# Ordinary products for the first four up chunks of a feed-forward stage, and norm sums added on VectorE

## The chip, the cores and the metric

The kernel runs on one core of a Trainium2 chip. The metric is the device time of one execution in microseconds (us). The kernel before takes 2769.68 us, the median of three runs (2767.59 to 2777.74). All durations below come from one profiled execution of it. TensorE is PE in the profile, VectorE is DVE, ScalarE is ACT, GpSimd is POOL, and SyncE, which issues the DMAs, is SP.

## The reference, cut to what matters

Two transformer blocks run one after the other, each two layers deep, on 512 tokens of width 1024, all in float32:

```
x = x + mixer(rms_norm(x, g_mix)) 
x = x + square(relu(rms_norm(x, g_ffn) @ w_ff1)) @ w_ff2     # 1024 -> 4096 -> 1024
rms_norm(x, g) = x * rsqrt(mean(x*x, axis=-1) + 1e-6) * g
```

The first block's mixer joins a pooling branch, a latent attention and a linear recurrence through gates (twice). The second block has a layer with retention and window attention ("even") and one with axial attention ("odd"). Each of the four layers ends in such a feed-forward stage (ffn), so there are four of them, and eight norms over the width.

## The kernel before

Activations lie transposed, 128 of the 1024 channels on the partitions and the 512 tokens along the row; `xs[d]` (tile `zg`) is the residual of channel chunk d. TensorE takes each float32 operand as a rounded part and a rest, `xh` and `xl` for activations, `h` and `lo` for weights, and `mm3` (L412 to L415) forms a product from three matmuls: hi by hi, hi by lo, lo by hi. A norm's factor is not multiplied into x ahead of the product: x times its gain is split at once (`split_x`), and the factor of each token is applied to the product.

**Weights** come as 439 slabs of 512 KB. `fetch` (L369 ff.) issues the DMA on SP into a raw buffer (three of them), ACT rounds it to `h` (L394) and DVE subtracts to get `lo` (L395); for 38 slabs POOL does that. `ahead` keeps three slabs fetched in front of the one in use.

**The norm's statistic.** `Sum.add` squares a chunk of x on ACT (L470) and adds it to `ssq` on POOL (L421, called from L474). `tokens` (L481) multiplies `ssq` with ones on TensorE, so that each token's sum lies on its own partition, and DVE scales it (`tm`, L484). `rsqrt` makes 1/sqrt by three Newton steps on DVE, eleven operations on 128x4. `bcast` turns the result into a row for all partitions: two rounded diagonal tiles (`ssp`, DVE, L418), two matmuls with ones (L514), a copy by ACT (L517, `r2b` in an ffn, `rb` in a mixer). In the mixers `getr` does the statistic and the broadcast in one call, inside the first products.

**The up product.** Up chunk f is 128 of the 4096 columns. An ordinary chunk (`gemm`) is 8 x 3 matmuls of 512 tokens. The ffn before never uses that: a `Pair` handles two chunks by seven half-size products p1 to p7 (a Winograd scheme of the 2x2 blocks: halves of the contraction by halves of the tokens), 7 x 4 x 3 = 84 matmuls of 256 tokens. It needs seven forms of the weights, made by `fetch_up` (L341: five splits `sh`, `sl` and four sums or differences on DVE, for each pair), and seven of x, made by `split_up` (L532) at the end of the product before the ffn (`w_out`, or the mixers' out-projection), together with that product's own additions (`zg`), the squares and the POOL adds. `xh` holds the first token half and a difference in its even chunks; `th`, `tl` hold three more forms.

**The order.** The ffn calls pairs 0 and 1 first, with `tokens` after the first four products of pair 0 and `bcast` among pair 1's, then per group of four chunks two pairs and four down slabs (`ff2`). `tc.high_priority(offset=60)` moves what it holds 60 steps forward. The scheduler writes one fixed queue for each engine when the kernel is built; each engine works its queue in order. Accumulators in PSUM: three `ps_acc`, two `ps_s`, two `ps_tr`, one `ps_o`.

Of the kernel before, what the change touches and what calls it, by code (L numbers as in the profile page):

```python
# [16 lines left out]
S = 512  # L17
D = 1024
# [281 lines left out]
def build(tc, a, upto=None):  # L300
# [35 lines left out]
    for i, sl in enumerate(plan):  # L336
        if sl[0] and sl[0][0] in ("w_ff1", "w_mlp_up_2") and i - 1 not in ups:
            ups[i] = True
    up = {}

    def fetch_up():  # L341
# [18 lines left out]
        for src in (a1, b1, s1, a2, b2):  # L360
            fh = up["p"].tile([P, 4, P], F32R, name="sh", bufs=8)
            fl = up["p"].tile([P, 4, P], F32R, name="sl", bufs=8)
# [44 lines left out]
    def ahead():  # L407
        while pos[0] < min(len(plan), pos[1] + AHEAD):
            fetch()
# [52 lines left out]
    class Sum:  # L462
# [4 lines left out]
        def add(self, src, scale=None, eng=None):  # L467
# [5 lines left out]
            if self.n:  # L473
                add(self.s, self.s, dst, eng or nc.gpsimd)  # L474
            self.n += 1

        def tokens(self, n, eps=EPS, tag="s"):

            t = ps(tag)
            for b in range(NB):  # L480
# [3 lines left out]
            nc.vector.tensor_scalar(m, t[:, 0:2 * NB].rearrange("p (b t) -> p b t", t=2)[:, :, 0], 1.0 / n, eps,  # L484
                                    op0=ALU.mult, op1=ALU.add)
# [5 lines left out]
    def rsqrt(m, n=NB):  # L491

        i, y, t = nrm.tile([P, n], I32, name="ti%d" % n, bufs=2), small("ty%d" % n, n), small("tt%d" % n, n)
# [10 lines left out]
    def bcast(cols, out=None, tag="o", name="rb"):  # L504

        hl = [nrm.tile([P, NB], F32R, name=n, bufs=2) for n in ("bh", "bl")]
        nc.vector.tensor_copy(hl[0], cols)
        nc.vector.tensor_sub(hl[1], cols, hl[0].bitcast(F32))
        dg = nrm.tile([P, 2, S], F32R, name="ssp")
        t = ps(tag)  # L510
        for i in range(2):
            mul(dg[:, i].rearrange("p (b t) -> p b t", b=NB), identb,
                hl[i].bitcast(F32)[:, :, None].to_broadcast([P, NB, P]))
# [3 lines left out]
        nc.scalar.activation(out, t, AF.Copy)  # L517
# [13 lines left out]

    def split_up(d, src, g, mk):  # L532

        i, odd_ = divmod(d, 2)
        x = mk()
        nc.scalar.activation(x, src, AF.Copy, scale=g)
        if not odd_:
            t = mk()  # L540
            nc.vector.tensor_sub(t[:, 0:H], x[:, H:], x[:, 0:H])
            split(xh[:, d, 0:H], xl[:, d, 0:H], x[:, 0:H])
            split(xh[:, d, H:], xl[:, d, H:], t[:, 0:H])
            up["even"] = (x, t)
            return
        xe, t = up["even"]
        split(xh[:, d], xl[:, d], x)
        t2 = mk()
        nc.vector.tensor_sub(t2[:, 0:H], x[:, H:], t[:, 0:H])
        nc.vector.tensor_sub(t2[:, H:], x[:, 0:H], t2[:, 0:H])  # L550
        nc.vector.tensor_sub(t[:, H:], x[:, H:], xe[:, H:])
        th, tl = up["th"][:, i], up["tl"][:, i]
        split(th[:, 1:3], tl[:, 1:3], t2.rearrange("p (a b) -> p a b", a=2))
        split(th[:, 0], tl[:, 0], t[:, H:])
# [23 lines left out]


    def ffn(n1, n2, l, xs, sq, after):  # L580

        with contextlib.ExitStack() as st:
# [20 lines left out]
            class Pair:  # L606
# [32 lines left out]
                def out(self):  # L639
                    r = rb[0]  # L640
                    for j, t in enumerate(self.t):
                        stt(t, t, 0.0, r, op0=ALU.max)
                        yf = tp.tile([P, S], F32, name="yf", bufs=2)
                        nc.scalar.activation(yf, t, AF.Square)
                        y = yp.tile([P, 2, S], F32R, name="y")
                        nc.scalar.activation(y[:, 0], t, AF.Square)  # L646
                        nc.vector.tensor_sub(y[:, 1], yf, y[:, 0].bitcast(F32))  # L647
                        ys[2 * self.p + j] = y
# [15 lines left out]
            ahead()  # L664
            a0.mm("p3")
            a1 = Pair(1)
            a1.mm("p1")
            a0.mm("p4")
            a1.mm("p6")
            with tc.high_priority(offset=60):  # L670
                rb.append(bcast(y, tag="acc", name="r2b"))
            a0.out()
            a1.mm("p7", "p5", "p3", "p2")
            ahead()
            nxt = Pair(2)
            nxt.mm("p1")
            a1.mm("p4")
            a1.out()
            for j in range(1, KF // 4 + 1):
                for e in range(2):  # L680
                    c = None
                    if j < KF // 4:
                        c = nxt or Pair(2 * j + e)
                        c.mm(*(("p6", "p7") if nxt else ("p1", "p6", "p7")))
                        nxt = None
                    ff2(j - 1, 2 * e)
                    if c:
                        c.mm("p5", "p3", "p2")
# [10 lines left out]
    def mixer1(l, getr, xsrc, xs, mkpool):  # L699
# [14 lines left out]
        with contextlib.ExitStack() as st:  # L714
# [259 lines left out]
        with contextlib.ExitStack() as st:  # L974
# [19 lines left out]
            for d in range(KD):  # L994
# [5 lines left out]
                split_up(d, xs[d], vc("g_ffn", 8 * l + d), mm_)  # L1000
# [134 lines left out]
    def even(getr, xs, finish):  # L1135
# [6 lines left out]
        with contextlib.ExitStack() as st:  # L1142
# [4 lines left out]
            with tc.high_priority(offset=60):  # L1147
                rb, later = getr()
# [14 lines left out]
            for h in range(RH):  # L1163
# [10 lines left out]
                for i in range(2):  # L1174
                    acc = gemm(slab(_gemm(e, 0, _rng(R_G + 256 * h + P * i))))
# [372 lines left out]
```

## Time and profile before

| what | us |
|---|---|
| median of three runs | 2769.68 |
| the profiled execution | 2771.13 |
| its span | 2769.3 |
| PE busy in the span | 2692.5 (97%) |
| DVE busy | 2079.8 (75%) |
| ACT busy | 1289.1 (47%) |
| POOL busy | 272.7 (10%) |

An engine's busy time is the union of its instructions' durations. PE's matmuls overlap in the trace, so the pace of a run of them is the distance between two starts, not a duration. The granted clock (PEclk in a view by windows) is 1.00 at TensorE's full clock of 2.4 GHz and 0.50 at 1.2 GHz; a mean between the two says what share of the window each level had. The ffn stages begin at about 370, 1088, 1848 and 2415 us, the second mixer of the first block at 716, the even layer at 1425, the odd one at 2205.

### The profile page before, as it was taken

Reading aid. Unit: us, or ns where it says so; the run is one execution under the profiler, and the core shown is the slowest. Engines: PE = TensorE matmul, PEld = TensorE weight load, DVE = VectorE, ACT = ScalarE, POOL = GpSimd, SP = SyncE. Lnnn points to the kernel's source line nnn. Section 1 sums busy time; section 2 is a strip of 40 time slices with the busy share of each in tenths; the row PEclk is TensorE's granted clock in tenths of the full one; section 3 lists DMA queues with packets and bytes.
Section 4 is the critical chain, followed back from the end, with each engine's and each line's share of the span. In section 5 each row is a group of like instructions: output and inputs, shape, how many; then the busy total and the mean of one; then the engine's idle time right before and its main releaser. Section 6 shows DMA issues by size and latency. Waiting matters only on the chain. (4 is left out here: it accounts for less than half of the span.)

```text
span 2769.3 us, 38564 instructions
## 1 busy us (share of the span) xinstructions
PE 2692.5 (97%) x14774; PEld 2307.0 (83%) x14774; DVE 2079.8 (75%) x3925; ACT 1289.1 (47%) x2112; POOL 272.7 (10%) x186
## 2 busy tenths in 40 slices
PE   8999999999999999999999989989999999999999
PEld 6887889999777778999978878869999877789998
DVE  8647798777775779887766665688788676798775
ACT  4437654343354675443443335564434346644332
POOL 0100010000110002000031112330000132300000
PEclk9999999999999999999999999999999999999999
DMA  4331433332434223323322222213332311132332
GB/s 160 105 109 54 130 105 109 103 103 92 127 112 147 73 85 121 122 92 108 106 76 83 82 71 74 70 46 119 102 99 94 98 62 38 39 107 92 108 106 69
DMA packets 80481, 262.88 MB, mean 95 GB/s; under 512 B 9223, under 2 KB 13063, under 8 KB 80296
## 3 DMA queue, kind: packets, MB, share of 16 engines
q1 hardware_dynamic: 80296, 260.41, 29.4%
q8 instruction: 116, 1.90, 0.3%
q14 instruction: 69, 0.57, 0.1%
HBM read 248.06 MB, written 12.32 MB: 94 GB/s over the span
## 5 line engine op out<-in xcount | busy, mean ns | idle before, releaser
L394 ACT ACTIVATE h<-w 128x1024 fp32r<-128x1024 f32 (+1 forms) x313 | 329.7, 1055 | 700.5 <-issue 287.8
L413 PE MATMUL ps_acc<-y,h 128*128 128x512 f32 x1024 | 399.6, 391 | 0.0
L415 PE MATMUL ps_acc<-y,lo 128*128 128x512 f32 x1024 | 399.4, 390 | 0.0
L414 PE MATMUL ps_acc<-y,h 128*128 128x512 f32 x1024 | 399.1, 390 | 0.0
L395 DVE TENSOR_TENSOR lo<-w,h 128x1024 fp32r<-128x1024 f32 (+1 forms) x275 | 342.0, 1245 | 45.8 <-ACT h L394 43.2
L421 DVE TENSOR_TENSOR zg<-zg,ps_acc 128x512 f32<-128x512 f32 x304 | 207.3, 684 | 194.6 <-PE ps_acc L415 194.4
L413 PE MATMUL ps_acc<-xh,h 128*128 128x512 f32 x752 | 302.3, 402 | 0.0
L415 PE MATMUL ps_acc<-xh,lo 128*128 128x512 f32 x752 | 302.3, 402 | 0.0
L414 PE MATMUL ps_acc<-xl,h 128*128 128x512 f32 x752 | 302.0, 402 | 0.0
L415 PEld LDWEIGHTS ps_acc<-y,lo 128*128 128x128 f32 x1024 | 192.2, 188 | 41.1
L413 PEld LDWEIGHTS ps_acc<-y,h 128*128 128x128 f32 x1024 | 192.5, 188 | 37.5 <-ACT y L646 1.1
L414 PEld LDWEIGHTS ps_acc<-y,h 128*128 128x128 f32 x1024 | 192.3, 188 | 36.7 <-DVE y L647 0.8
L421 POOL TENSOR_TENSOR ssq<-ssq,sq 128x512 f32<-128x512 f32 x55 | 103.1, 1874 | 974.9 <-ACT sq L470 516.3
L413 PE MATMUL ps_tr<-xh,h 128*128 128x256 f32 (+1 forms) x544 | 166.8, 307 | 15.6 <-ACT xh L429 8.5
L414 PE MATMUL ps_tr<-xl,h 128*128 128x256 f32 (+1 forms) x544 | 165.7, 305 | 6.8 <-DVE xl L430 6.8
L430 DVE TENSOR_TENSOR sl<-w,sh 128x512 fp32r<-128x512 f32 x256 | 168.8, 682 | 3.6 <-ACT sh L429 3.4
L415 PEld LDWEIGHTS ps_acc<-xh,lo 128*128 128x128 f32 x752 | 143.5, 191 | 32.3 <-issue 1.7
L413 PEld LDWEIGHTS ps_acc<-xh,h 128*128 128x128 f32 x752 | 143.4, 191 | 32.2 <-issue 1.9
L414 PEld LDWEIGHTS ps_acc<-xl,h 128*128 128x128 f32 x752 | 143.6, 191 | 30.9 <-issue 0.8
L415 PE MATMUL ps_tr<-xh,lo 128*128 128x256 f32 (+1 forms) x544 | 166.5, 306 | 0.1
L429 ACT ACTIVATE sh<-w 128x512 fp32r<-128x512 f32 x256 | 151.1, 619 | 29.2 <-DVE w L357 15.2
L414 PE MATMUL ps_s<-tl,sh 128*128 128x256 f32 x480 | 136.5, 284 | 0.7 <-DVE tl L430 0.7
(422 smaller groups left out, 6671.6 us busy)
## 6 DMA issues: line engine op xcount, KB each, us to landing
w<-w SPq DMA_DIRECT2D x439, 512.0 KB, 3.6
md<-gz SPq DMA_DIRECT2D x16, 256.0 KB, 2.5
m<-md SPq DMA_DIRECT2D x16, 256.0 KB, 4.1
x0t<-xT SPq DMA_DIRECT2D x8, 256.0 KB, 6.4
m<-xT SPq DMA_DIRECT2D x8, 256.0 KB, 3.8
xd<-zg SPq DMA_DIRECT2D x8, 256.0 KB, 2.1
m<-xd SPq DMA_DIRECT2D x8, 256.0 KB, 3.9
out<-zg SPq DMA_DIRECT2D x8, 256.0 KB, 2.0
```

Source lines behind the costliest of these rows:

```text
L394: nc.scalar.activation(h[:, c], w[:, c], AF.Copy)
L395: (nc.gpsimd if idle(i) else nc.vector).tensor_sub(lo[:, c], w[:, c], h[:, c].bitcast(F32))
L413: nc.tensor.matmul(out, w[0], x[0], start=first, stop=False)
L414: nc.tensor.matmul(out, w[0], x[1], start=False, stop=False)
L415: nc.tensor.matmul(out, w[1], x[0], start=False, stop=last)
L421: (eng or nc.vector).tensor_add(out, x, y)
L429: nc.scalar.activation(hi, src, AF.Copy)
L430: nc.vector.tensor_sub(lo, src, hi.bitcast(F32))
```

## The change

It has four parts.

1. **Chunks 0 to 3 of each ffn are ordinary products.** Two chunks by `gemm2` (two accumulators side by side), one `gemm`, the broadcast, one more `gemm`. The pairs begin with pair 2. `split_up` is gone: the product before an ffn ends with the plain `split_x`. The forms of x are made by `forms` while the four chunks run, and at last the difference is written over the second token half of the even chunks of `xh`, `xl`.
2. **Pair 2's slabs are held back** (`up["hold"]`) until the second chunk has been squared; the rings `sh` and `sl` have 7 buffers, not 8; in the later rounds p5 comes ahead of the first down slab.
3. **`Sum.add` adds on DVE.** The 55 adds of `ssq` and 4 of `sqq` leave POOL; 7 of another sum (`sg`) stay there.
4. **Statistic and broadcast apart.** `getr` ends with the Newton steps; `bcast` is called later: after the fourth product in the first block's mixer, and in the even layer after two products for the gates of head 0 that are moved up for this. In the odd layer the broadcast, whose result nobody read, is gone. The small DVE operations, the diagonals and ACT's copy run at high priority.

```diff
@@ ffn_plan
-    out = up(0) + up(1)
+    out = [_gemm(n1, l, _rng(f * P)) for f in range(4)]
@@ ahead
-        while pos[0] < min(len(plan), pos[1] + AHEAD):
+        while pos[0] < min(len(plan), pos[1] + AHEAD) and not (up.get("hold") and pos[0] in ups):
@@ Sum.add
-                add(self.s, self.s, dst, eng or nc.gpsimd)
+                add(self.s, self.s, dst, eng)
@@ bcast
-        nc.vector.tensor_copy(hl[0], cols)
-        nc.vector.tensor_sub(hl[1], cols, hl[0].bitcast(F32))
         dg = nrm.tile([P, 2, S], F32R, name="ssp")
+        with tc.high_priority(offset=60):
+            nc.vector.tensor_copy(hl[0], cols)
+            nc.vector.tensor_sub(hl[1], cols, hl[0].bitcast(F32))
+            for i in range(2):
+                mul(dg[:, i].rearrange("p (b t) -> p b t", b=NB), identb,
+                    hl[i].bitcast(F32)[:, :, None].to_broadcast([P, NB, P]))
@@ ffn
+            def forms(i):
+                e, o = xs[2 * i], xs[2 * i + 1]
+                ge, go = gx(2 * i), gx(2 * i + 1)
+                half = lambda name, bufs: tp.tile([P, H], F32, name=name, bufs=bufs)
+                t1 = half("t1", 4)
+                nc.vector.tensor_sub(t1, e[:, H:], e[:, 0:H])
+                nc.scalar.activation(t1, t1, AF.Copy, scale=ge)
+                e2 = half("m1", 2)
+                nc.scalar.activation(e2, e[:, H:], AF.Copy, scale=ge)
+                t = tp.tile([P, S], F32, name="t", bufs=4)
+                stt(t[:, 0:H], o[:, H:], go, t1, op1=ALU.subtract)
+                stt(t[:, H:], o[:, 0:H], go, t[:, 0:H], op1=ALU.subtract)
+                t3 = half("u2", 2)
+                stt(t3, o[:, H:], go, e2, op1=ALU.subtract)
+                split(th[:, i, 1:3], tl[:, i, 1:3], t.rearrange("p (a b) -> p a b", a=2))
+                split(th[:, i, 0], tl[:, i, 0], t3)
+                return t1
...
-            a0 = Pair(0)
-            a0.mm("p1", "p5", "p2", "p6")
-            with tc.high_priority(offset=60):
-                y = rsqrt(sq.tokens(D, tag="acc"))
-            a0.mm("p7")
...
+            up["hold"] = True
+            ws = [slab(_gemm(n1, l, _rng(f * P))) for f in range(2)]
+            accs = gemm2(*ws)
+            y = rsqrt(sq.tokens(D))
+            t1s = [forms(0)]
+            accs.append(gemm(slab(_gemm(n1, l, _rng(2 * P)))))
+            rb.append(bcast(y, name="r2b"))
+            for f in range(4):
+                if f == 1:
+                    accs.append(gemm(slab(_gemm(n1, l, _rng(3 * P)))))
+                if f:
+                    t1s.append(forms(f))
+                t = tp.tile([P, S], F32, name="t", bufs=4)
+                stt(t, accs[f], 0.0, rb[0], op0=ALU.max)
+                square(f, t)
+                if f == 1:
+                    up["hold"] = False
+                    ahead()
+            for i, t1 in enumerate(t1s):
+                split(xh[:, 2 * i, H:], xl[:, 2 * i, H:], t1)
@@ mixer1
-            with tc.high_priority(offset=60):
-                rb = getr()
+            y = getr()
             accs.append(gemm(slab(slab_in(l, POOL0 + P))))
+            rb = bcast(y)
@@ even
-            with tc.high_priority(offset=60):
-                rb, later = getr()
+            gate = lambda h, i: gemm(slab(_gemm(e, 0, _rng(R_G + 256 * h + P * i))))
+            gacc = [gate(0, 0)]
+            y, later = getr()
+            gacc.append(gate(0, 1))
+            rb = bcast(y)
@@ odd
-        with tc.high_priority(offset=60):
-            rb, later = getr()
+        rt_, later = getr()
```

The queues of three places follow. DVE, at the first ffn's broadcast, before (`w_3457`, `w_3458` and the `sl` are the weight forms of pair 2, `ssp` the diagonals, `t_3400` a result of pair 0):

```order
577 L358 TENSOR_TENSOR w_3457<-w_3457 128x512
578 L507 CAST bh_3548<-ty4_3428 128x4
579 L421 TENSOR_TENSOR u2_3546<-ps_s_3533,m1_3517 128x256
580 L430 TENSOR_TENSOR sl_3471<-w_3457,sh_3470 128x512
581 L508 TENSOR_TENSOR bl_3549<-ty4_3428,bh_3548 128x4
582 L430 TENSOR_TENSOR sl_3475<-w_3458,sh_3474 128x512
583 L418 TENSOR_TENSOR ssp_3552<-ident_85,bh_3548 128x512
584 L430 TENSOR_TENSOR sl_3479<-s1_3464,sh_3478 128x512
585 L418 TENSOR_TENSOR ssp_3552<-ident_85,bl_3549 128x512
586 L430 TENSOR_TENSOR sl_3483<-w_3457,sh_3482 128x512
```

And now, in the changed kernel (`sl_3458` is the last weight form of pair 2, `lo_3582` the rest of the second down slab, `xl_88` the difference written over `xl`):

```order
550 L430 TENSOR_TENSOR sl_3458<-w_3429,sh_3457 128x512
551 L418 TENSOR_TENSOR tt4_3312<-ty4_3311 128x4
552 L395 TENSOR_TENSOR lo_3582<-w_3580,h_3581 128x1024
553 L424 SCALAR_TENSOR_TENSOR tt4_3312<-tt4_3312,tm_3308 128x4
554 L430 TENSOR_TENSOR xl_88<-t1_3324,xh_87 128x256
555 L424 SCALAR_TENSOR_TENSOR ty4_3311<-tt4_3312,ty4_3311 128x4
556 L430 TENSOR_TENSOR xl_88<-t1_3407,xh_87 128x256
557 L514 CAST bh_3363<-ty4_3311 128x4
558 L430 TENSOR_TENSOR xl_88<-t1_3467,xh_87 128x256
559 L515 TENSOR_TENSOR bl_3364<-ty4_3311,bh_3363 128x4
560 L418 TENSOR_TENSOR ssp_3365<-ident_85,bh_3363 128x512
561 L418 TENSOR_TENSOR ssp_3365<-ident_85,bl_3364 128x512
```

Before, only weight forms and sums of finished products stand between the Newton steps; now the rest of a slab that is still to be fetched stands there too, ahead of both diagonals.

PE at the same broadcast, before (`ps_acc_3553` takes the broadcast, `ps_s_3605` a product of pair 1):

```order
1760 L414 MATMUL ps_s_3605<-xl_88,sh_3301 128x256
1761 L415 MATMUL ps_s_3605<-xh_87,sl_3302 128x256
1762 L514 MATMUL ps_acc_3553<-ssp_3552,ones_83 128x512
1763 L413 MATMUL ps_s_3605<-xh_87,sh_3301 128x256
1764 L414 MATMUL ps_s_3605<-xl_88,sh_3301 128x256
```

And now (`ps_acc_3382` is chunk 3, `ps_s_3532` the first product of pair 2):

```order
1713 L414 MATMUL ps_acc_3382<-xl_88,h_3248 128x512
1714 L521 MATMUL ps_o_3370<-ssp_3365,ones_83 128x512
1715 L415 MATMUL ps_acc_3382<-xh_87,lo_3249 128x512
1716 L521 MATMUL ps_o_3370<-ssp_3365,ones_83 128x512
1717 L413 MATMUL ps_s_3532<-th_2918,sh_3441 128x256
1718 L414 MATMUL ps_s_3532<-tl_2919,sh_3441 128x256
1719 L415 MATMUL ps_s_3532<-th_2918,sl_3442 128x256
```

The broadcast stood among the products of pair 1; it now stands one matmul before the end of the four ordinary chunks, and pair 2 comes behind it.

PE at the start of the even layer, before (`ps_s_13818` is the statistic, `ps_tr` the first two products; the statistic of the other sum stands a few rows above):

```order
7504 L481 MATMUL ps_s_13818<-onesf_81,sg_10183 128x1 x4
7505 L415 MATMUL ps_tr_13745<-xh_87,lo_13575 128x512
7506 L413 MATMUL ps_tr_13745<-xh_87,h_13574 128x512
7507 L414 MATMUL ps_tr_13745<-xl_88,h_13574 128x512
7508 L415 MATMUL ps_tr_13745<-xh_87,lo_13575 128x512
7509 L413 MATMUL ps_tr_13746<-xh_87,h_13624 128x512
```

And now, some products later (`ps_acc_13661` and `ps_acc_13689` are the first two accumulators of the values, which follow the two gates in the three `ps_acc` buffers):

```order
7459 L1032 MATMUL ps_acc_13661<-lo_13501,xh_87 128x256
7460 L1033 MATMUL ps_acc_13661<-h_13500,xl_88 128x256
7461 L1031 MATMUL ps_acc_13689<-h_13444,xh_87 128x256
7462 L1032 MATMUL ps_acc_13689<-lo_13445,xh_87 128x256
7463 L1033 MATMUL ps_acc_13689<-h_13444,xl_88 128x256
```

The statistic no longer stands inside the first product; the second accumulator of the values now takes the buffer of the first gate, which is free once DVE has multiplied that gate with the broadcast.

## Rows read from the trace of the kernel before

**Rows 1.** The page, part 1: busy us, share, instructions
```profile
PE 2692.5 (97%) x14774; PEld 2307.0 (83%) x14774; DVE 2079.8 (75%) x3925; ACT 1289.1 (47%) x2112; POOL 272.7 (10%) x186
```
**Rows 2.** By windows: width, PE, PEld, DVE, ACT, POOL busy, PEclk, DMA share, GB/s
```profile
365.00:390.00 25.00, 21.79 (x150) 19.85 (x150) 24.28 (x53) 12.56 (x24) 4.07 (x3) 1.00 0.27 94
500.00:525.00 25.00, 25.00 (x166) 22.98 (x165) 19.90 (x32) 10.06 (x16) 0.00 (x0) 1.00 0.27 90
700.00:725.00 25.00, 21.87 (x94) 17.67 (x93) 21.63 (x37) 10.21 (x15) 8.49 (x6) 0.93 0.56 179
1085.00:1110.00 25.00, 22.45 (x162) 21.35 (x161) 23.91 (x54) 12.10 (x24) 2.72 (x2) 0.93 0.15 45
1425.00:1450.00 25.00, 18.45 (x69) 15.14 (x68) 17.23 (x45) 9.29 (x14) 13.34 (x9) 0.73 0.16 53
1836.00:1850.00 14.00, 11.17 (x51) 8.74 (x49) 14.00 (x23) 10.07 (x19) 5.29 (x4) 1.00 0.21 75
1850.00:1875.00 25.00, 17.17 (x82) 15.69 (x83) 23.80 (x54) 11.61 (x23) 8.85 (x3) 0.66 0.13 43
2200.00:2225.00 25.00, 22.35 (x120) 19.06 (x119) 16.35 (x33) 7.78 (x12) 5.63 (x5) 0.93 0.21 64
2400.00:2425.00 25.00, 18.87 (x93) 15.88 (x91) 24.91 (x42) 16.80 (x32) 16.81 (x6) 0.93 0.12 43
2425.00:2450.00 25.00, 22.12 (x134) 20.28 (x135) 22.19 (x52) 12.16 (x22) 1.73 (x2) 0.73 0.27 85
```
**Rows 3.** Waits of PE, whole span: total us, times, longest
```profile
PE ps_s L481 <- POOL ssq L421: 12.3, 3, 6.5
PE ps_acc L481 <- POOL ssq L421: 4.5, 4, 3.2
```
**Rows 4.** Waits of PE, 1836 to 1880
```profile
PE ps_tr L413 <- ACT xh L429: 4.5, 2, 2.7
```
**Rows 5.** Timeline of PE: start, us, engine, line, operation
```profile
500.40 0.28 PE L413 MATMUL ps_s<-th,sh 128*128 128x256 f32 x1
...
504.81 0.28 PE L414 MATMUL ps_tr<-tl,sh 128*128 128x256 f32 x1
```
**Rows 6.** Timeline of PE at the start of the second mixer
```profile
730.06 0.40 PE L413 MATMUL ps_acc<-xh,h 128*128 128x512 f32 x1
...
740.97 0.40 PE L415 MATMUL ps_acc<-xh,lo 128*128 128x512 f32 x1
```
**Rows 7.** By lines: count, busy us, mean ns, idle before
```profile
L421 POOL TENSOR_TENSOR ssq<-ssq,sq 128x512 f32<-128x512 f32 x55 | 103.1, 1874 | 974.9 <-ACT sq L470 516.3
L421 DVE TENSOR_TENSOR zg<-zg,ps_acc 128x512 f32<-128x512 f32 x304 | 207.3, 684 | 194.6 <-PE ps_acc L415 194.4
```
**Rows 8.** Timeline of DVE, SP and ACT, 528 to 535, a slab's way
```profile
528.79 1.28 DVE L430 TENSOR_TENSOR sl<-w,sh 128x512 fp32r<-128x512 f32 x2
...
529.50 0.33 SPq L393 DMA_DIRECT2D w<-w  x1
...
532.59 1.06 ACT L394 ACTIVATE h<-w 128x1024 fp32r<-128x1024 f32 x1 [4.06 <-issue]
...
533.68 1.23 DVE L395 TENSOR_TENSOR lo<-w,h 128x1024 fp32r<-128x1024 f32 x1 [0.22 <-ACT h L394]
```
**Rows 9.** Timeline of DVE, and a POOL row, before the second mixer's broadcast
```profile
715.22 0.75 DVE L424 SCALAR_TENSOR_TENSOR xl<-zg,vec,xh 128x512 fp32r<-128x512 f32 x1 [0.79 <-ACT xh L432]
...
717.99 1.34 POOL L421 TENSOR_TENSOR ssq<-ssq,sq 128x512 f32<-128x512 f32 x1 [0.86 <-ACT sq L470]
...
718.13 1.74 DVE L424 SCALAR_TENSOR_TENSOR xl<-zg,vec,xh 128x512 fp32r<-128x512 f32 x1
721.16 0.16 DVE L484 TENSOR_SCALAR tm<-ps_s 128x4 f32<-128x4 f32 x1 [1.29 <-PE ps_s L481]
...
724.42 0.68 DVE L418 TENSOR_TENSOR ssp<-ident,bl 128x512 fp32r<-128x512 f32 x1
```

More of the change, by code (lines that the diff above doesn't have):

```diff
@@ L336, in build @@
     for i, sl in enumerate(plan):
-        if sl[0] and sl[0][0] in ("w_ff1", "w_mlp_up_2") and i - 1 not in ups:
+        if sl[0] and sl[0][0] in ("w_ff1", "w_mlp_up_2") and sl[1][2][0] == 2 * P and i - 1 not in ups:
             ups[i] = True
@@ L491, in rsqrt, with newton @@
     def rsqrt(m, n=NB):
+        with tc.high_priority(offset=60):
+            return newton(m, n)
+    def newton(m, n):
         i, y, t = nrm.tile([P, n], I32, name="ti%d" % n, bufs=2), small("ty%d" % n, n), small("tt%d" % n, n)
@@ L516, in bcast @@
             out = nrm.tile([P, S], F32, name=name)
-        nc.scalar.activation(out, t, AF.Copy)
+        with tc.high_priority(offset=60):
+            nc.scalar.activation(out, t, AF.Copy)
         return out
@@ L530, in open_up @@
         up["tl"] = up["p"].tile([P, NB, 3, H], F32R, name="tl")
[L532 to L554, printed above, removed]
     soft = cpool.tile([P, 12], F32, name="soft")
@@ L577, in softplus, with ffn @@
         nc.vector.tensor_scalar_mul(soft4[:, 4:8], soft[:, 0:4], 8.0)
-    def ffn(n1, n2, l, xs, sq, after):
+    def ffn(n1, n2, l, xs, sq, after, gx):
         with contextlib.ExitStack() as st:
@@ L999, in mixer1 @@
                 add(xs[d], acc, xt)
-                split_up(d, xs[d], vc("g_ffn", 8 * l + d), mm_)
+                split_x(d, xs[d], vc("g_ffn", 8 * l + d))
                 sq.add(xs[d])
@@ L1174, in even @@
                 for i in range(2):
-                    acc = gemm(slab(_gemm(e, 0, _rng(R_G + 256 * h + P * i))))
+                    acc = gacc[i] if h == 0 else gate(h, i)
                     f = mk("gs")
@@ L1257, in even @@
         open_up()
-        with contextlib.ExitStack() as st:
-            fp = pool("fin", 1, st)
-            outproj("w_out_even_2", 12, sw[4:8], xs, finish(lambda: fp.tile([P, S], F32, name="m", bufs=6)))
+        outproj("w_out_even_2", 12, sw[4:8], xs, finish)
         outer.close()
@@ L1266, in odd @@
         accs = gemm2(w0, slab(_gemm(o, 0, ax_cols(D + P))))
-        with tc.high_priority(offset=60):
-            rb, later = getr()
+        rt_, later = getr()
         outer = contextlib.ExitStack()
@@ L1321, in odd @@
         open_up()
-        with contextlib.ExitStack() as st:
-            fp = pool("fin", 1, st)
-            outproj("w_out_odd_2", 4, oTs[4:8], xs, finish(lambda: fp.tile([P, S], F32, name="m", bufs=6)))
+        outproj("w_out_odd_2", 4, oTs[4:8], xs, finish)
         outer.close()
@@ L1393, in build @@
     xsrc = a["xT"]
-    getr = lambda sq=sq: bcast(rsqrt(sq.tokens(D)))
+    getr = lambda sq=sq: rsqrt(sq.tokens(D))
     for l in range(2):
@@ L1409, in after @@
                 sq.add(xs[d])
-            ffn("w_ff1", "w_ff2", l, xs, sqf, after)
+            ffn("w_ff1", "w_ff2", l, xs, sqf, after, lambda d: vc("g_ffn", 8 * l + d))
             stx.close()
             xsrc = xd
-            getr = lambda sq=sq: bcast(rsqrt(sq.tokens(D)))
+            getr = lambda sq=sq: rsqrt(sq.tokens(D))
         else:
@@ L1421, in after @@
                 sq.add(xs[d])
-                sg.add(xs[d], vc("g_final", d))
-            ffn("w_ff1", "w_ff2", l, xs, sqf, after)
+                sg.add(xs[d], vc("g_final", d), nc.gpsimd)
+            ffn("w_ff1", "w_ff2", l, xs, sqf, after, lambda d: vc("g_ffn", 8 * l + d))
         if upto == ("ffn", l):
@@ L1431, in getr2 @@
         r1 = small("tr%d" % NB)
-        mul(r1, y1, y1)
         m = sg.tokens(D, 0.0)
-        mul(m, m, r1)
-        nc.vector.tensor_scalar_add(m, m, EPS)
-        y = rsqrt(m)
-        mul(rt[:, 0:NB], y, y1)
-        mul(rt[:, NB:], rt[:, 0:NB], rt[:, 0:NB])
-        rb = bcast(rt[:, 0:NB])
+        with tc.high_priority(offset=60):
+            mul(r1, y1, y1)
+            mul(m, m, r1)
+            nc.vector.tensor_scalar_add(m, m, EPS)
+            y = rsqrt(m)
+            mul(rt[:, 0:NB], y, y1)
+            mul(rt[:, NB:], rt[:, 0:NB], rt[:, 0:NB])
         def later():
@@ L1444, in later, with finish @@
                 stt(xs[d], xs[d], vc("g_final", d), r1b)
-        return rb, later
+        return rt[:, 0:NB], later
     for l in range(2):
         sq = Sum()
-        def finish(mk):
-            def f(d):
-                split_up(d, xs[d], vc("norm_mlp_2", 8 * l + d), mk)
-                sq.add(xs[d])
-            return f
+        def finish(d):
+            split_x(d, xs[d], vc("norm_mlp_2", 8 * l + d))
+            sq.add(xs[d])
         (even if l == 0 else odd)(getr2, xs, finish)
@@ L1468, in after @@
                 nc.sync.dma_start(out[:, d], xs[d])
-        ffn("w_mlp_up_2", "w_mlp_down_2", l, xs, sq, after)
+        ffn("w_mlp_up_2", "w_mlp_down_2", l, xs, sq, after, lambda d: vc("norm_mlp_2", 8 * l + d))
         if upto == ("ffn2", l):
@@ L1476, in getr2 @@
                 y = rsqrt(sq2.tokens(D))
-                nc.vector.tensor_copy(rt[:, 0:NB], y)
-                mul(rt[:, NB:], y, y)
-                return bcast(y), lambda: None
+                with tc.high_priority(offset=60):
+                    nc.vector.tensor_copy(rt[:, 0:NB], y)
+                    mul(rt[:, NB:], y, y)
+                return y, lambda: None
     assert pos[1] == len(plan)
```

49 lines of the change are left out of this document (17 added, 32 removed).

## The prediction

> **What bounds the kernel now.** I began with the page's busy times [rows 1]. PE is busy for 97% of the span, so the kernel can gain only where PE stands still or runs at half its clock, and it loses whatever work PE is given on top. DVE has 75%, and that average hides short stretches in which it has no room. So the next view was the span cut into windows [rows 2]. In the middle of an ffn, 500 to 525, PE is busy for the whole window at clock 1.00 with DVE at 19.9 of 25 us: nothing is lost there. The losses sit where one norm gives way to the next product. I price a window as the time in which PE was not busy plus (1 - PEclk) times its width, since a matmul at half clock takes twice as long. At the four ffn starts that gives 3.2 us (365 to 390), 2.55 + 1.75 = 4.3 (1085 to 1110), 2.83 + 7.83 + 8.5 = 19.2 (1836 to 1875) and 6.13 + 1.75 + 2.88 + 6.75 = 17.5 (2400 to 2450), together 44.2 us. DVE is busy for 22 to 25 of 25 us in all of them. The second mixer loses 3.13 + 1.75 = 4.9 (700 to 725), the even layer 6.55 + 6.75 = 13.3 (1425 to 1450), the odd layer 2.65 + 1.75 = 4.4 (2200 to 2225). The view of PE's waits says for what: 12.3 + 4.5 us of statistic matmuls waiting for POOL's last add [rows 3], of which 6.5 at once in the even layer, and in the third ffn the splits of x on ACT [rows 4].
>
> **Part 1, products.** An ordinary pair of chunks is 48 matmuls of 512 tokens. Just such a pair runs at the second mixer's start: 47 steps in 10.91 us [rows 6], 0.232 each, so 11.1 us. A Winograd pair is 84 matmuls of 256: 37 steps in 4.41 us [rows 5], 0.119 each, so 10.0 us. Eight pairs change, +1.1 each: **+9.0 us** on PE, which nothing covers.
>
> **Part 1, the ffn starts.** What waits now is gone: seven forms of x no longer stand between the last out-projection and the first product, and DVE and ACT have about 22 us of ordinary products to make them. What comes late instead is the broadcast. Count from the end of the last out-projection. PE does two chunks in 11.1 us, then the four small statistic matmuls, then two more chunks; its first broadcast matmul stands one matmul before their end, at +22.2. DVE gets the statistic at +11.3. In the queue the Newton steps are threaded between the weight forms of pair 2 and, just ahead of the diagonals, a `lo` of the second down slab. Up to the last reader of pair 2's first raw buffer, DVE has two `lo` (1.2 each [rows 8]), two differences and four `sl` (0.6 each) and nine small operations. Alone, a small one is 0.19 (14 in 2.66 us ahead of the diagonals [rows 9]), threaded in between some 0.15: 2.4 + 3.6 + 1.4 = 7.4, so +18.7. Only then is a raw buffer free for that slab. How long it takes from there stands in the trace [rows 8]: a buffer's last reader ends at 529.47 on DVE (half way between two `sl`, which end at 530.07), the DMA is issued at 529.50, ACT rounds at 532.59, DVE starts the `lo` at 533.68: 4.2 us. So the `lo` can start at +22.9, while DVE is there at +19.5 and stands for 3.4 us. Behind it wait, in order, three splits of half width (0.4 each by the same pace), the rest of the small operations (0.9) and the first diagonal: 22.9 + 1.15 + 1.2 + 0.9 + 0.6 = +26.7 at most; some of these steps overlap, I take +26.4. PE then waits 26.4 - 22.2 = **4.2 us**. Bounds: 1.0 if the slab is there on time (DVE without its 3.4 us pause), 8 if ACT is late too, whose copy of the broadcast stands behind the rounding of pair 2's weights, itself behind the fourth chunk. Thereafter DVE has about 11 us of forms, outputs and squares for about 9 us of PE's products up to the last one that needs `tl`: another 0 to 2 us, I take 0.5. The clock: of the windows with 2.5 to 3.2 us of idle time, three show 0.93 and one 1.00 [rows 2], so 1.75 us each. Sum for each ffn 4.2 + 0.5 + 1.75 = 6.4, for four 25.8 against 44.2 now: **-18.4**. The first two get worse (by 3.2 and 2.1), the last two better by 12.8 and 11.1.
>
> The rule for the clock in the Trainium skill ("TensorE: Matmul & The Clock Gate", Part 1) speaks against this change: a TensorE that stands still is put back to the lower of its two levels, so trading many short waits for one long one may cost more than the wait. The trace agrees for three of the four windows named. By the rule in all four stages and for two such stretches each, the sum would be 7 us higher, a third of the way to rival B below.
>
> **Part 2** I cost at nothing: in steady rounds the forms are made a round ahead and DVE has 5 of 25 us free in the window of 500 to 525 [rows 2]; with p5 earlier a ring of 7 turns as fast as one of 8. If that cover is gone, one late `sl` of 0.6 in each of 28 later pairs is 17 us, my upper bound.
>
> **Part 3.** 59 adds go from POOL (1874 ns on average) to DVE, where an add of that shape takes 684 [rows 7]: +40 us of DVE work, spread over the whole span and hidden except at the ends of stages. There the add's way shortens by 1.2 us, and it stops pressing on its neighbour: the split at 718.13 took 1.74 us beside POOL's add at 717.99, the same split at 715.22 took 0.75 [rows 9]. So the moved add (0.68) costs DVE less than the collision did (1.0).
>
> The Trainium skill ("SBUF — State Buffer", SBUF: two separate sides) says that VectorE and GpSimd share one port pair and that the loser is shut out for the whole instruction. By the trace it agrees [rows 9]: 1.74 is 0.75 and 1.0 of waiting. By the rule alone all 59 moves would gain DVE 0.3 us or more; I count only those at stage ends.
>
> **Part 4.** Second mixer: the statistic now has another chunk ahead of it and the broadcast one more, so the 4.9 us go and perhaps 1 comes back: **-3.9**. Odd layer: the 4.4 go, with two broadcast matmuls of 0.23: **-4.9**. Even layer: the 13.3 go, but the second accumulator of the values takes the first gate's buffer, which is freed by a DVE product with the broadcast. PE is there after two products, two gates and one half-wide value: 11.1 + 5.6 + 5.6 + about 4.5 = +27. The broadcast: statistic at about +17, two Newton chains and their joining (some 30 small operations, 5.7), five or six slabs' `lo` between them (6.5), diagonals 1.3, copy and product 2 to 3: +33 to +34. That is a wait of 7, 1.4 more for the broadcast matmul, and 3.5 of half clock: 11.9 in place of 13.3. Bounds 3 and 17; I take **-1**. The norms of the heads keep their shape: **-1**, from 7 to either side, since 38 slabs stay on POOL.
>
> **The sum.** +9.0 - 18.4 - 3.9 - 4.9 - 1 - 1 = -20.2. From the profiled execution, 2771.1 us (its span 2769.3 and 1.8 around it), that gives 2750.9; the median of the runs shown lies 1.4 lower, so I predict **2749 us**.
>
> **Rivals.** With L for the loss at each ffn start, the time is 2771.1 - 1.4 + 9.0 - 44.2 - 10.8 + 4L = 2723.7 + 4L.
>
> *A: the slab comes in time.* If the raw buffer is freed earlier or the `lo` is off the broadcast's way, L is 1 to 2: 2728 to 2732, and with the even layer's full gain about 2720. For it: PE itself is then the only bound, and DMA is idle for three quarters of the window. Against it: the buffer is read last by a form that stands behind the Newton steps.
>
> *B: the new waits eat the gain.* L near 10, from a wait of 5 to 6 and a long half-clock stretch as at 2425 to 2450 (6.75 us) [rows 2]: 2764, no change that shows. For it: the wait falls at one place on PE with nothing to fill it.
>
> *C: slower, DVE becomes the bound of the ffn starts.* The late diagonals push the outputs of four chunks, the forms of x and the splits of the even chunks behind them, and pair 2 waits once more for `tl`, in all four stages. If each loses what the third loses today (19.2), the time is 2800. It decides from L = 11.5 (no gain) and shows as slower from L = 15. For it: DVE is busy for 24 of 25 us there today, with fewer operations moved in. Against it: the forms of two weight pairs and `split_up` leave that stretch, more work than comes.
>
> *D: it does not do what it says:* the wait moves but nothing overlaps, since the scheduler threads the Newton steps between others anyway; then L stays at 11 as now and the products cost 9: 2768, with B.
>
> **Chances.** Mine 0.5 (2738 to 2758), A 0.18, B and D 0.22, C 0.1. A measurement of this kernel can tell about 0.5% from no change, 13.8 us: faster is below 2755.8, slower above 2783.5. Faster: A, and most of mine (0.47): 0.65. Same: B, D, the rest of mine, a part of C: 0.27. Slower: 0.08. The range reaches from A's lower middle to B's end: 2727 to 2771.
>
> **What would show it.** Right: no wait of the statistic for POOL; in each ffn PE waiting 3 to 6 us for `ssp` at the broadcast, with DVE's idle time just before the `lo` ahead of it; the windows of the third and fourth ffn at 0.93 or better; a wait for the first gate's accumulator in the even layer. Wrong: no idle time at that broadcast (A), waits for `tl` or `xl` in pair 2 of over 3 us (C), idle time of PE in the steady rounds (part 2), or clock 0.73 in the windows of all four ffn (B).

## The result and the profile after

The changed kernel takes 2728.76 us (median of four runs, 2726.02 to 2731.43) against 2770.36 of the kernel before beside it; the ratio is 0.9846, 95% interval 0.9824 to 0.9867. The gain of 41.6 us is twice the 20.7 that I had forecast, and the time lies where rival A stood.

The page, part 1, after (columns as in [rows 1]):

```profile
PE 2675.7 (98%) x14484; PEld 2279.0 (84%) x14484; DVE 2030.2 (74%) x3860; ACT 1276.3 (47%) x2071; POOL 165.8 (6%) x127
```

PE is busy for 16.8 us less than before, the span is 42.9 shorter. The windows of the changed kernel that answer to [rows 2] (ffn starts at 369.6, 1080.3, 1838.1 and 2381.7, the second mixer at 709.5, the even layer at 1420.2, the odd at 2177.9):

```profile
365.00:390.00 25.00, 25.00 (x114) 20.46 (x113) 20.81 (x45) 15.36 (x29) 0.00 (x0) 1.00 0.22 66
388.00:413.00 25.00, 25.00 (x143) 21.53 (x142) 23.97 (x52) 14.44 (x26) 0.00 (x0) 1.00 0.20 70
700.00:725.00 25.00, 25.00 (x110) 20.36 (x109) 16.02 (x26) 10.07 (x14) 0.00 (x0) 1.00 0.56 179
1080.00:1105.00 25.00, 25.00 (x114) 20.08 (x113) 22.12 (x53) 16.15 (x30) 0.00 (x0) 1.00 0.34 107
1430.00:1455.00 25.00, 18.34 (x98) 15.37 (x96) 16.71 (x47) 5.83 (x7) 1.26 (x1) 0.95 0.25 85
1840.00:1865.00 25.00, 25.00 (x123) 20.53 (x122) 20.99 (x49) 13.05 (x24) 0.00 (x0) 1.00 0.33 106
2165.00:2190.00 25.00, 25.00 (x115) 20.56 (x113) 17.27 (x25) 11.46 (x18) 0.00 (x0) 1.00 0.26 85
2380.00:2405.00 25.00, 25.00 (x114) 20.21 (x112) 21.73 (x51) 13.52 (x25) 0.00 (x0) 1.00 0.31 103
```

All four ffn starts are full now, at clock 1.00, the broadcast in the second row among them. DVE has 1 to 4 us free in 25 where it had 0 to 3. Of the starts only the even layer's still loses nearly what it did.

So that stages can be compared although they move, I cut each trace at two kinds of matmul in PE's timeline: the last one of the product before an ffn, and the last down product of that ffn. Lengths in us:

| stage | before | after | difference | forecast |
|---|---|---|---|---|
| first mixer | 363.8 | 362.2 | -1.6 | 0 |
| ffn 1 | 341.4 | 339.9 | -1.5 | +5.4 |
| second mixer | 374.1 | 370.8 | -3.3 | -3.9 |
| ffn 2 | 341.9 | 339.9 | -2.0 | +4.4 |
| even layer | 418.8 | 417.9 | -0.9 | -1 |
| ffn 3 | 354.3 | 339.7 | -14.6 | -10.5 |
| odd layer | 212.2 | 203.9 | -8.3 | -4.9 |
| ffn 4 | 351.5 | 340.6 | -10.9 | -8.9 |

(The forecast of an ffn is its products, +2.25, and 6.4 less its loss of before; -1 for the heads' norms isn't placed.) The four ffn give 29.0 us where I had 9.6. That is nearly the whole miss.

PE's waits of the changed kernel (total us, times, longest) hold no statistic that waits for a sum, as against [rows 3]:

```profile
PE ps_s L521 <- DVE ssp L418: 8.8, 4, 4.0
PE ps_o L521 <- DVE ssp L418: 7.5, 6, 4.2
PE ps_tr L413 <- ACT h L394: 7.4, 1, 7.4
PE ps_acc L1031 <- DVE gs L418: 7.1, 1, 7.1
```

The first two rows are the norms of heads and keys, not the ffn's; the longest of the second, 4.2 us in the odd layer, was 1.9 before, so there the change costs something. The third is the program's first weight. The fourth is the wait for the first gate's accumulator that I had forecast, with 7; what makes it is not what I had counted (see part 4 below).

### The profile page after: what moved, and what is told of

Read it like the earlier page. It is cut to its first block, busy times and chain, and to the rows that moved or that the text cites. A ratio compares the mean times of both kernels' runs of the same rounds, so it can differ in the third digit from the quotient of the medians.

```text
span 2726.4 us, 37828 instructions
## 1 busy us (share of the span) xinstructions
PE 2675.7 (98%) x14484; PEld 2279.0 (84%) x14484; DVE 2030.2 (74%) x3860; ACT 1276.3 (47%) x2071; POOL 165.8 (6%) x127
## 4 chain that ended last, share of the span: by engine, by line
PE 90%; DVE 6%; ACT 1%; POOL 1%; issue 1%; DMA 0%; SPq 0%; POOLq 0%; DVEq 0%; ACTq 0%
PE ps_acc L415 18%; PE ps_acc L413 18%; PE ps_acc L414 18%; PE ps_tr L415 4%; PE ps_tr L413 4%; PE ps_tr L414 4%; PE ps_s L413 3%; PE ps_s L414 3%; PE ps_s L415 3%; PE ps_o L413 1%; PE ps_o L415 1%; PE ps_o L414 1%; PE ps_tr L956 1%; POOL rp L421 1%; PE ps_acc L1031 1%
## 5 line engine op out<-in xcount | busy, mean ns | idle before, releaser
L394 ACT ACTIVATE h<-w 128x1024 fp32r<-128x1024 f32 (+1 forms) x329 | 346.7, 1055 | 724.8 <-PE ps_acc L414 416.5
L413 PE MATMUL ps_acc<-xh,h 128*128 128x512 f32 x816 | 328.1, 402 | 0.0
L415 PE MATMUL ps_acc<-xh,lo 128*128 128x512 f32 x816 | 327.9, 402 | 0.0
L414 PE MATMUL ps_acc<-xl,h 128*128 128x512 f32 x816 | 326.4, 400 | 0.0
L413 PE MATMUL ps_tr<-xh,h 128*128 128x256 f32 (+1 forms) x592 | 184.2, 311 | 8.0 <-ACT h L394 7.4
L415 PE MATMUL ps_tr<-xh,lo 128*128 128x256 f32 (+1 forms) x592 | 183.9, 311 | 0.0
L414 PE MATMUL ps_tr<-xl,h 128*128 128x256 f32 (+1 forms) x592 | 182.6, 309 | 0.0
L430 DVE TENSOR_TENSOR sl<-w,sh 128x512 fp32r<-128x512 f32 x224 | 147.6, 682 | 0.0
L415 PE MATMUL ps_s<-th,sl 128*128 128x256 f32 x448 | 126.6, 283 | 0.0
L413 PE MATMUL ps_s<-th,sh 128*128 128x256 f32 x448 | 126.5, 282 | 0.0
```

The lines of the kernel that those rows point to most:

```text
L394: nc.scalar.activation(h[:, c], w[:, c], AF.Copy)
L413: nc.tensor.matmul(out, w[0], x[0], start=first, stop=False)
L414: nc.tensor.matmul(out, w[0], x[1], start=False, stop=False)
L415: nc.tensor.matmul(out, w[1], x[0], start=False, stop=last)
L430: nc.vector.tensor_sub(lo, src, hi.bitcast(F32))
```

## The experiments

Each kernel ran on the chip beside the kernel before; a ratio is to that one, with its 95% interval. The kernel before took 2770 to 2776 us in the four sets of runs, so a few us between kernels of different sets prove little.

### Undoing and isolating the parts

**Adds on POOL again** (the changed kernel):

```diff
-                add(self.s, self.s, dst, eng)
+                add(self.s, self.s, dst, eng or nc.gpsimd)
```

> The changed kernel with one part undone: the sums of squares are added on POOL again. Theory 1 (the gain comes from taking the forms of x out of the product before each ffn; the adds matter little once 11 us of product stand ahead of the statistic): 0 to +5 us on the changed kernel's 2728.8, the ffn stages stay at 340 us. Rival (the sums leaving POOL are the gain): PE waits for POOL's last add again, 10 us or more in all, and the ffn starts lose 3 us or more each: +15 to +25.

Measured: 2728.76 us, ratio 0.9849 (0.9824 to 0.9874), the same as the changed kernel. The ffn stages are 339.8, 339.9, 339.7 and 339.8. POOL's timeline of this kernel at the first ffn shows why; the stage begins at 370.5:

```profile
374.22 1.53 POOL L421 TENSOR_TENSOR ssq<-ssq,sq 128x512 f32<-128x512 f32 x1 [4.87 <-ACT sq L470]
```

The last add ends at 375.75, some 6 us before the statistic is due behind two chunks. With the ordinary chunks and the parting there, it is late no more on either engine.

**Adds on DVE alone** (the kernel before):

```diff
-                add(self.s, self.s, dst, eng or nc.gpsimd)
+                add(self.s, self.s, dst, eng)
...
-                sg.add(xs[d], vc("g_final", d))
+                sg.add(xs[d], vc("g_final", d), nc.gpsimd)
```

> The kernel before with one part of the change alone: the sums of squares are added on DVE. Theory 1: the waits for POOL (16.8 us) go, but the forms of x stay in front of the ffn and DVE, at 24 of 25 us there, gets the adds on top: -3 to -10 us on the kernel before. Rival (the adds are the gain): -25 us or more.

Measured: 2754.95 us, ratio 0.9932 (0.9918 to 0.9947), 19 us under the kernel before beside it: between the two theories. By stages most of it is in the odd layer (-6.2), ffn 3 (-5.6), the second mixer (-4.6) and ffn 4 (-3.9); ffn 1 and 2 lose 2.7 and 0.8, the even layer 4.6. What stays is the splits of x: in the third ffn PE waits 5.2 us for `xh`.

**Adds and the parting of statistic and broadcast, without the ordinary chunks** (the kernel before with parts 3 and 4; against the changed kernel:)

```diff
-            ws = [slab(_gemm(n1, l, _rng(f * P))) for f in range(2)]
-            accs = gemm2(*ws)
...
+            a0 = Pair(0)
+            a0.mm("p1", "p5", "p2", "p6")
...
```

> The kernel before with the adds on DVE and the statistic and broadcast apart, but with the seven-product pairs from the start of each ffn, as before. Theory 1: the four ffn stages keep most of their loss (together 30 to 44 us against the changed kernel's, less the 9 us that its products cost more), so 2745 to 2760. Rival (ordinary products are a cost of 9 us and no more): 2720 to 2725.

Measured: 2759.66 us, ratio 0.995 (0.9935 to 0.9965), at the upper end of theory 1 and slower than the adds alone. The ffn stages are 344.0, 341.8, 348.6 and 347.7, 22 us more than the changed kernel's, although their products should take PE 8 to 9 us less.

**Statistic and broadcast together again** (the changed kernel without part 4; of its edits, the one in the first block's mixer):

```diff
-            y = getr()
+            with tc.high_priority(offset=60):
+                rb = getr()
             accs.append(gemm(slab(slab_in(l, POOL0 + P))))
-            rb = bcast(y)
```

> The changed kernel with the statistic and the broadcast in one call and at their old places and priorities again (mixer, even and odd layer), ffn as changed. Theory 1 (each stage's part stands by itself): the starts of the second mixer, the even and the odd layer lose again, without POOL's waits, +4 to +10. Rival (the odd layer's and mixer's gains come from the adds alone): 0 to +2.

Measured: 2722.42 us, ratio 0.9818 (0.9803 to 0.9832). Both theories had the wrong sign: 6 us faster than the changed kernel. So it was run again beside it.

> The changed kernel itself, once more beside the next one on the same chip, to tell a few us apart: 2726 to 2731 by theory 1 and by its rival.

> The changed kernel with statistic and broadcast together again, repeated with more rounds beside the changed kernel. Theory 1b (keeping them apart costs: broadcasts later, a wait for the gate's accumulator in the even layer, one for the odd layer's key norm): 4 to 7 us under the changed kernel. Rival (the two are the same, and the difference seen was scatter): within 2 us.

Measured on one chip: 2729.16 us (2725.99 to 2732.81) for the changed kernel, 2723.07 (2720.97 to 2724.68) without part 4; ratios 0.9831 (0.9817 to 0.9846) and 0.9809 (0.9794 to 0.9823). Theory 1b holds by its number: 6.1 us, and the two sets of runs don't overlap. By stages the second mixer gains 2.9, the even layer 2.9, the odd one 3.7 in this pair of profiles, 1.5, -0.8 and 0.8 in the first pair; which part of part 4 costs them is not settled. PE's waits name two places: with part 4 it waits 7.1 us for the gate's accumulator in the even layer, without it 3.6 for the last add of the statistic, and in the odd layer 4.2 against 2.0 for the diagonals of the key norm. This version beats both kernels.

**The ordinary chunks alone** (the kernel before with parts 1 and 2; against the kernel without part 4 it is this line):

```diff
-                add(self.s, self.s, dst, eng)
+                add(self.s, self.s, dst, eng or nc.gpsimd)
```

> The kernel before with the ordinary chunks, the plain split and the forms made during them, and nothing else: sums on POOL, statistic and broadcast as before. Theory 1 (the forms of x in front of the ffn were the loss, and the other two parts add nothing to that): 2722 to 2730, ffn stages 340 us, less than 5 us of waiting for POOL's sums in the odd and even layers. Rival (each part is needed where the other leaves a hole: without the adds on DVE the mixers' statistics wait for POOL again, 12 us): 2735 to 2745.

Measured: 2739.42 us, ratio 0.9869 (0.9852 to 0.9885), in the rival's range. Its ffn stages are 339.9, 339.9, 339.8 and 340.6: the ffn gain is whole without parts 3 and 4 (parts 1 and 2 were not taken apart). What lacks is in the mixers, in PE's waits of this kernel:

```profile
PE ps_s L481 <- POOL ssq L421: 12.3, 3, 6.5
```

The same row as in [rows 3]: the odd layer, the even one and the second mixer still wait for POOL. So parts 3 and 4 are two remedies for one wait: with the ordinary chunks there, the adds alone take 16 to 17 us off, both together 10, and the parting alone, in another set, about as much as both.

| ordinary chunks | adds on DVE | apart | us |
|---|---|---|---|
| | | | 2770 to 2776 |
| | x | | 2755.0 |
| | x | x | 2759.7 |
| x | | | 2739.4 |
| x | | x | 2728.8 |
| x | x | | 2722.4, 2723.1 |
| x | x | x | 2728.8, 2729.2 |

### The prices

**Eight ordinary chunks** (the changed kernel; chunks 4 to 7 by `gemm` in the first round, forms written at its end):

```diff
-                    if j < KF // 4:
+                    if j == 1:
+                        for f in (4 + 2 * e, 5 + 2 * e):
+                            acc = gemm(slab(_gemm(n1, l, _rng(f * P))))
...
+                    elif j < KF // 4:
```

> The changed kernel with the first eight up chunks of each ffn as ordinary products, not four; nothing of its starts is changed. It measures the price of a pair by itself: eight more pairs at 11.14 - 10.01 = 1.13 us each. Theory 1: +9 us (8 to 10), the ffn stages 342.2 us. Rival (the steady rounds also gain or lose by the lighter DVE): 0 to +4, or +14 and more.

Measured: 2741.46 us, ratio 0.9875 (0.9851 to 0.9898), +12.7, between theory 1 and its rival. Every ffn stage is 341.7, 1.9 above the changed kernel's where that one has no idle time, so a pair costs 1.9 / 2 = 0.9 to 1.0 us, 7 to 8 for eight pairs: a little under my 1.13. The rest, some 6 us, is in the mixers (even layer +3.7, second mixer +1.6, odd +1.4), whose code is the same; PE had 48 us at half clock there, 37.5 in the changed kernel's profile.

**A late broadcast** (the changed kernel; each diagonal of the ffn's broadcast written four times):

```diff
-            for i in range(2):
+            for i in [0, 1] * (extra + 1):
...
-            rb.append(bcast(y, name="r2b"))
+            rb.append(bcast(y, name="r2b", extra=3))
```

> The changed kernel with the two diagonals of each ffn's broadcast written four times over, 3.6 us more of DVE ahead of the broadcast: as long as the pause of 3.4 us that I had forecast there. The planner puts 15 matmuls of pair 2 (1.8 us) ahead of the broadcast for it. Theory 1 (the broadcast has next to no slack, so a pause would have cost what I said, and it is the pause that did not happen): PE waits 1.5 to 2 us for the diagonals and 1 to 2 us more in pair 2, with a half clock in some stages: +10 to +18. Rival (PE has slack there and would have hidden such a pause): 0 to +4.

Measured: 2747.08 us, ratio 0.9896 (0.9873 to 0.992), +18.3, just above theory 1's range. In PE's timeline of this kernel:

```profile
397.72 1.10 PE L521 MATMUL ps_o<-ssp,ones 128*128 128x512 f32 x2 [1.44 <-DVE ssp L418]
399.50 0.58 PE L413 MATMUL ps_o<-xh,sh 128*128 128x256 f32 x1 [0.69 <-ACT r2b L525]
```

The ffn stages are 2.8 to 4.0 us longer: 2.2 us of waits in each, and in three of four half clock behind them (the window of 385 to 410 is at 0.93). There is next to no slack at that place. So the price I set on a pause was right in kind, and the pause was not there.

**A late slab** (the changed kernel; one column of the first down slab's raw buffer is read behind pair 2's last form):

```diff
+                    nc.vector.tensor_sub(small("keep", 1), up["w"][:, 0, 0:1], slabs[pos[1]]["b2"][1][:, 0, 0:1].bitcast(F32))
```

> The changed kernel with one more read of the first down slab's raw buffer, one column on DVE, that can't come before pair 2's last weight form: the second down slab's transfer then starts 4 us later, as I had forecast it. The planner answers by placing that slab's rest behind the diagonals, not ahead. Theory 1 (the wait needs both: a late buffer and the rest ahead of the diagonals in the queue): 0 to +3 us on the changed kernel, no wait at the ffn's broadcast. Rival (a late buffer alone brings the wait, at the broadcast or at the second down slab): +10 to +25.

Measured: 2744.77 us, ratio 0.9889 (0.9874 to 0.9904), +15.6: by the number the rival. By the trace not: PE has no idle time over 0.1 us in any ffn and clock 1.00, nothing waits. The transfer of the second down slab is issued at 390.44 in the first ffn, +19.1, when the fourth form of pair 2 has left its buffer: that is the release that I had forecast, at +18.7. The slab's `lo` then runs at 395.04, behind both diagonals. Each ffn is 2 to 3 us longer because its down products are slower. By lines, this kernel, whose lines stand one further down, and then the changed one (count, busy us, mean ns):

```profile
L416 PE MATMUL ps_acc<-y,lo 128*128 128x512 f32 x1024 | 404.2, 395 | 0.0
```

```profile
L415 PE MATMUL ps_acc<-y,lo 128*128 128x512 f32 x1024 | 399.9, 390 | 0.0
```

From start to start it is 232.3 ns against 228.0; 3072 such matmuls make 13 us. The buffer was late and the broadcast did not wait, so a late buffer alone is not enough, as theory 1 said. That late buffer and queue order together would bring the wait is not shown: no kernel had both. The small tile brought an effect of its own, most likely by moving the tiles that come after it in memory (the last section has what speaks for it); no run moved a tile by itself.

**The even layer's statistic earlier:**

```diff
-            gacc = [gate(0, 0)]
             y, later = getr()
+            gacc = [gate(0, 0)]
```

> The changed kernel with the even layer's statistic asked for ahead of the first gate, not behind it. The layer's wait of 7.1 us for the first gate's accumulator hangs on the chain statistic, Newton, broadcast. Theory 1 (the chain starts 5.6 us later than it could): the wait falls to 1 to 3 us and the half clock behind it goes: -5 to -9. Rival (the chain's length on DVE and POOL's seven adds decide, or the rotated queries and keys are late next): 0 to -2.

Measured: 2728.45 us, ratio 0.9828 (0.98 to 0.9856): nothing, as the rival said. The statistic comes earlier, yet PE's wait for the gate is 6.3 us. DVE's timeline of this kernel shows what stands in between:

```profile
1448.55 1.29 DVE L418 TENSOR_TENSOR tab<-tab,rb 128x512 f32<-128x512 f32 x2
1449.76 3.51 DVE L418 TENSOR_TENSOR rp<-ps_tr,tab 128x512 f32<-128x512 f32 x5
...
1455.37 1.29 DVE L418 TENSOR_TENSOR gs<-ps_acc,rb 128x512 f32<-128x512 f32 x2
```

The broadcast is there before 1448.55, but the gate's product, which frees the accumulator, stands behind the scaling of the tables and the rotation of queries and keys in DVE's queue.

**Two ordinary chunks** (the changed kernel; pair 1 by seven products behind two chunks):

```diff
-    out = [_gemm(n1, l, _rng(f * P)) for f in range(4)]
+    out = [_gemm(n1, l, _rng(f * P)) for f in range(2)] + up(1)
...
+            c = Pair(1)
+            c.mm("p1", "p2", "p3")
+            t1s = [forms(i) for i in range(4)]
+            c.mm("p6", "p7")
```

> The changed kernel with only two ordinary up chunks in each ffn, pair 1 by seven products straight after (those that need plain x first), broadcast behind its fifth product. It saves four pairs, 4.5 us. Theory 1 (the four chunks' 22 us are what covers DVE's forms; 11 us are not enough): PE waits for th and tl, 4 us or more in each ffn, +5 to +20 with half clocks. Rival (half the cover is enough): -4.5, a better kernel.

Measured: 2755.3 us, ratio 0.9925 (0.9901 to 0.9949), +26.5, above theory 1's range. The ffn stages are 347.3, 348.0, 344.0 and 344.7. No wait is long: by PE's waits in the first ffn the longest is 0.8 us and the sum 3.0; in the first two the clock falls besides (windows of this kernel):

```profile
370.00:395.00 25.00, 23.21 (x129) 19.30 (x127) 24.00 (x59) 16.81 (x34) 0.00 (x0) 0.97 0.27 85
395.00:420.00 25.00, 23.83 (x131) 21.45 (x131) 23.05 (x42) 10.79 (x19) 0.00 (x0) 0.83 0.23 75
```

DVE is the pace here, with 23 to 24 of 25 us. Four chunks are enough to cover its forms; two, in this arrangement, are not.

## Why the prediction was right in direction and half in size

**The step that failed** is the broadcast of the ffn: "Only then is a raw buffer free for that slab", at +18.7, and the 3.4 us in which DVE "stands" for the second down slab's rest, priced with what follows at 6.4 us per ffn. Measured: no wait there. In the four ffn stages together PE stands still for 0.6 us, and its clock is 1.00 throughout, so L is 0.15 in place of 6.4. With that my own formula gives 2724. The measured time is 5 us above it, about as much as I had priced the loss before too high (below). The timeline of the changed kernel at the first ffn (DVE, SP and PE; the stage begins at 369.6):

```profile
383.31 1.22 DVE L395 TENSOR_TENSOR lo<-w,h 128x1024 fp32r<-128x1024 f32 x1
384.55 0.33 SPq L393 DMA_DIRECT2D w<-w  x1
389.34 1.22 DVE L395 TENSOR_TENSOR lo<-w,h 128x1024 fp32r<-128x1024 f32 x1
392.13 0.68 DVE L418 TENSOR_TENSOR ssp<-ident,bh 128x512 fp32r<-128x512 f32 x1
392.96 0.47 PE L521 MATMUL ps_o<-ssp,ones 128*128 128x512 f32 x1
```

The slab's transfer starts at +14.9, in the moment in which the first down slab's `lo` ends (384.53), not behind pair 2's forms, the last of which ends at 389.36. I had let the three raw buffers turn in a ring; the buffer taken is the one that is free first, which the down slab before it leaves after a single use (in the program the two slabs lie in the same place). The `lo` then runs at +19.7, where I had DVE arrive at +19.5, without a pause; the first diagonal ends at +23.2 and PE comes for it at +23.3. The rest of my count was good to about 1 us: the statistic's matmuls, which I had counted at nothing, take 0.8 us on PE, so statistic and broadcast come at +12.4 and +23.3 where I had +11.3 and +22.2. The whole result hung on the one release that I had inferred by counting and not read. The late slab says more: there the release is the one that I had counted, and the planner puts the `lo` behind the diagonals; so a pause that a count by hand finds right ahead of a critical step is a reason to doubt the count. The late diagonals show that the place itself has next to no slack: such a pause, had it been there, would have cost 3 to 4 us with the planner's answer to it.

That 2728.8 lies in my range is owed to the width of the range, which reached down into A's; by my own mechanism I had expected 2738 to 2758.

**Products:** +9.0 forecast; 0.9 to 1.0 a pair by the eight chunks, so 7 to 8. Right in kind, a little high.

**What goes at the ffn starts:** right, since all of it went, but priced too high. Of the 44.2 us, 2.5 lie ahead of the four stages, in the even and the odd layer (1.2 before 1847, 1.3 before 2414), and 3.3 are half clock that I priced where PE stood idle anyway. That leaves 38.4; the stages' lengths say 29.0 + 7.6 + 0.6, some 37. DVE's forms fit beside the four chunks; with two chunks, half the cover, each ffn is 4 to 8 us longer.

**Part 2:** no run has it by itself. PE is full in the steady rounds, so my zero holds beside part 1. My upper bound counted 28 later pairs; there are 14 in each ffn, 56 in all, so it should have been 34 us.

**The clock rule of the Trainium skill** ("TensorE: Matmul & The Clock Gate", Part 1) did not come to bear at the ffn starts, since PE hardly stood still there (0.6 us, in the fourth). The late diagonals agree with it in three stages of four: with the same 2.2 us of waits, 25 us around the broadcast are at 0.93 in the first, second and fourth ffn and at 1.00 in the third.

**Part 3:** I gave the adds a place at stage ends only, and that was right, but I set no term for them in the sum. By themselves they are worth 19 us in the kernel before. With the ordinary chunks and with statistic and broadcast apart they are worth nothing. The 40 us that DVE has more to do cost nothing that shows.

**Part 4:** -9.8 forecast. The second mixer (-3.3) and the odd layer (-8.3) got their gains, but not from this part: without it they are 369.3 to 369.8 and 201.7 to 203.1 us long, shorter still, and with the adds there part 4 costs 6 us. I had booked one wait once, rightly, but on the wrong edit. In the even layer the numbers were right, 7.1 of wait for a forecast of 7 and -0.9 for -1, but by luck. I had the broadcast come at +33 to +34; it is there at +28, as in these rows of the changed kernel (the layer begins at 1420.2):

```profile
1447.58 0.60 ACT L525 ACTIVATE rb<-ps_o 128x512 f32<-128x512 f32 x1 [1.96 <-PE ps_o L521]
...
1455.03 1.29 DVE L418 TENSOR_TENSOR gs<-ps_acc,rb 128x512 f32<-128x512 f32 x2
```

What fills the 7 us between is the scaling of the tables and the rotation of queries and keys on DVE, which the count left out; so the statistic earlier gained nothing.

Of the rivals, A came true, by a freer buffer as it said, though the even layer's gain, its other half, did not. The sum of 2749 was 20 too high: 25 by the term of the broadcast, less some 5 by which the other terms were too favourable, the price of the loss before above all.

## What to carry to other kernels

When a forecast hangs on the moment in which a buffer comes free, read from the queue or the trace which instruction releases it; a ring that is counted by hand can be wrong where buffers are reused by their release. When several edits aim at the same wait, take each away by itself: the sum of their gains is more than the wait, and one of them may only cost. Dearer products on a full TensorE can pay if they are what covers the work that made it wait, and only for as long as that work lasts.

## What the runs showed of the hardware that I had not expected

The same matmul of 512 columns with `y` takes 228.0 ns from start to start in the changed kernel, within 0.2 of that in every other one, and 232.3 in the one with a small tile more, at clock 1.00 and without a wait: 13 us on 3072 of them. Both paces stand side by side in every kernel. In the changed one, products of `y`, `yo` and `mg` (the activations of the down products and of two out-projections) start every 226.8 to 228.0 ns, those of `xh`, `xl` and `oT` every 232.6 to 232.7. With the small tile `y`, `yo` and `mg` go to 232.3 or 232.4, two others, `pp` and `lp`, go the other way, from 232.3 and 232.5 to 229.5 and 229.7, and `xh`, `xl` and `oT` stay within 0.5. That goes with the place of the tile in the program: the faster ones begin at a multiple of 256 bytes in their partition, the slower ones 128 bytes past one, and the small tile, three buffers of 128 bytes, pushes what comes after it 384 bytes on. Small groups agree less well (`rs`, 88 starts, does not change). No run moved a tile on purpose, so the cause is not shown; if it is this, moving `xh` and `xl` by 128 bytes could be worth some 11 us (an estimate: 2448 matmuls at 4.6 ns).

PE's half clock moved between profiles of stages whose code was the same: 10.2 and 13.7 us at half clock in the second mixer in two profiles of the changed kernel, with its length 370.8 and 372.7.
